# Side-by-side high and low halves in the activation tiles, and a fifth of the expert chunks loaded to two of those tiles

## The chip, the cores and the metric

The kernel runs on one core of one Trainium2 chip. The metric is the device time of one execution in microseconds (us); lower is better. Four engines do the work: TensorE (PE in the rows; its weight loads, which overlap the matmuls, are PEld), VectorE (DVE), ScalarE (ACT) and GpSimd (POOL). SyncE (SP) issues nearly all loads from HBM.

## The reference, cut to what matters

The reference is a stack of three transformer layers over 256 tokens of width 1024, all in fp32. The first two layers each mix three branches (a recurrent one, an mLSTM and attention to a memory) and end in a feed-forward part. The first of these is dense. The second is a mixture of 8 experts of which each token uses two:

```python
def swiglu(x, w1, w3, w2):            # dense; D_FF = 3584
    return (silu(x @ w1) * (x @ w3)) @ w2

# mixture: the same with w1[e], w3[e], w2[e] for the tokens sent to expert e,
# weighted by the gate and added back to their tokens
```

The third layer has two more dense feed-forward parts (width 2816) around a mixer with two kinds of attention. Every weight is used once per execution, so some 640 MB come from HBM.

## The kernel before, in words

**High and low parts.** Every fp32 matmul is made of fp32r products. A value is split into a high part (the value rounded to fp32r) and a low part (what is left). A product is high by high, plus high by low, plus low by high: three matmuls into one PSUM tile (`mm3`, lines 361 to 363).

**Weights.** They come in chunks of up to 128 x 2048 fp32, 1 MB, listed in the order of use. `run` goes through a list of steps. Each step names its chunks and a function `fn` that does its work. SP loads a chunk into a tile `w` of the pool `stream`, of which there are `RAW_BUFS` = 4 (line 317). `do_split` then casts it on ACT to the high part `wh` (line 330) and subtracts on DVE to get the low part `wl` (through `tt`, line 366). There are 3 tiles `wh` and 3 tiles `wl`. A chunk may be split up to 2 chunks ahead of the step that uses it (`look`). `load` issues the load of chunk n+4 as soon as the code has reached the split of chunk n; on the chip SP then waits until the subtraction of chunk n has read its `w`. The engines work in program order, and SP issues its loads in order.

**Activations.** They are kept with features on the partitions and the 256 tokens (`T`) along the free dimension. A tile `d` of the pool `act` (`t4k`, 4 KB a partition, 18 tiles) holds two groups of 128 features, k0 and k1, as `[P, 2, 512]`: high k0, high k1, low k0, low k1, 256 columns each. `HL` gives the two halves of such a tile, `fx` one group's high or low part.

**Three kinds of matmul groups.**
- `zmm`, `zmm_tok` and the small products use `mm3` with 256 moving columns.
- `wide` (dense feed-forward, gates, output projections) takes two matmuls a group. Line 474 has the high weights stationary and 512 moving columns, the high and the low part of one group k as `t[:, :, k*256:(k+1)*256]`: two runs of 256 columns that stand 512 columns apart. Line 476 (473 in the last group) has the low weights stationary and 256 moving columns.
- The experts (`moe_pass`) use `mm3` with the gathered tokens stationary and 512 weight columns moving, 12 matmuls a chunk. There are 8 experts x 7 blocks x 6 chunks = 336 chunks. Beside them stand the transposes (line 1349), the gathering of tokens (`prep`, lines 1297 to 1309, four times) and the scattering back (`scatter`, lines 1376 and 1377, eight times), whose sums go to `X` on DVE.

During the experts the pool of `d` tiles holds the tokens `x` (4 tiles, until the last `prep`), the gathered `xg` (4, and 8 around a `prep`), `sel`, the transposed products `ht` and the outputs `ys`.

Of the kernel before, what the change touches and what calls it, by code (L numbers as in the profile page):

```python
# [9 lines left out]
F32 = mybir.dt.float32  # L10
F32R = mybir.dt.float32r
# [3 lines left out]
OP = mybir.AluOpType  # L15
# [3 lines left out]
P = 128  # L19
# [211 lines left out]
class Step:  # L231

    look = LOOK

    def __init__(self, chunks, fn, fine=False, hold=False):
        self.chunks = chunks
        self.fn = fn
        self.fine = fine  # L240
        self.hold = hold


class HL(tuple):


    def __new__(cls, t):
        x = tuple.__new__(cls, (t[:, 0, :], t[:, 1, :]))
        x.t = t
        return x  # L250


class Kernel:
# [18 lines left out]
        return self.act.tile([P, 512], F32, name=self.name("a"), tag="a", bufs=10)  # L272

    def t4k(self, dt):
        return self.act.tile([P, 2, 512], dt, name=self.name("d"), tag="d", bufs=18)

    def pair(self):
        return HL(self.t4k(F32R))
# [1 line left out]
    def half(self, key):  # L280

        t = self.open.pop(key, None)
        if t is None:
            t = self.open[key] = self.t4k(F32)
            return t[:, 0, :]
        return t[:, 1, :]

    def t1k(self, dt=F32):
        return self.act.tile([P, 256], dt, name=self.name("b"), tag="b", bufs=6)
# [5 lines left out]
    def run(self, steps, small=False, before=lambda i, j: None):  # L295

        nc = self.nc
        flat = [c for s in steps for c in s.chunks]  # L300
        fine = [s.fine for s in steps for c in s.chunks]
        raw, split = [], []
        ns = 0

        def parts(i):
            e = flat[i].shape[-1]
            w = 512 if small or fine[i] else CHUNK
            return [slice(o, min(o + w, e)) for o in range(0, e, w)]

        def load():  # L310
            while not small and len(raw) < min(len(flat), ns + RAW_BUFS):
                ap = flat[len(raw)]
                e = ap.shape[-1]
                t = self.stream.tile([P, 2048], F32, name=self.name("w"), tag="w", bufs=RAW_BUFS)[:, :e]
                for j, s in enumerate(parts(len(raw)) if fine[len(raw)] else [slice(0, e)]):
                    before(len(raw), j)
                    nc.sync.dma_start(t[:, s], ap[:, s])
                raw.append(t)

        def do_split():  # L320
            e = flat[ns].shape[-1]
            hi, lo = (self.stream.tile([P, CHUNK], F32R, name=self.name(n), tag=n, bufs=SPLIT_BUFS)[:, :e]
                      for n in ("wh", "wl"))
            for s in parts(ns):
                if small:
                    t = self.t2k()
                    nc.sync.dma_start(t, flat[ns][:, s])
                else:
                    t = raw[ns][:, s]
                nc.scalar.copy(hi[:, s], t)  # L330
                self.tt(lo[:, s], t, hi.bitcast(F32)[:, s], OP.subtract)
            split.append((hi, lo))
            if not small:
                raw[ns] = None

        holds, n = [], 0
        for s in steps:
            if s.hold:
                holds.append(n)
            n += len(s.chunks)  # L340
        used = 0
        for s in steps:
            if s.hold:
                holds.pop(0)
            need = used + len(s.chunks)
            look = min(len(flat), need + s.look - 1, *holds[:1]) if s.chunks else 0
            load()
            while ns < look:
                do_split()
                ns += 1  # L350
                load()
            got = split[used:need]
            for i in range(used, need):
                split[i] = None
            used = need
            s.fn(*got)
# [22 lines left out]

    def split(self, src, hi, lo, scale=None):  # L380

        if scale is None:
            self.nc.scalar.copy(hi, src)
            self.tt(lo, src, hi.bitcast(F32), OP.subtract)
        else:
            self.actf(hi, src, AF.Identity, scale=scale)
            self.stt(lo, src, scale, hi.bitcast(F32), OP.mult, OP.subtract)

    def split_pair(self, src, hi, lo, scales):

        halves = [slice(m * T, (m + 1) * T) for m in range(2)]
        for s, c in zip(halves, scales):
            self.actf(hi[:, s], src[:, s], AF.Identity, scale=c)
        for s, c in zip(halves, scales):
            self.stt(lo[:, s], src[:, s], c, hi.bitcast(F32)[:, s], OP.mult, OP.subtract)

    def split2k(self, src, scale=None):
        x = self.pair()
# [64 lines left out]
    def wide(self, w, x, p, m=0, nk=DK, cols=256, koff=0, first=True, last=True):  # L463


        hi, lo = w
        for k in range(nk):
            o = k * cols + m * P
            a, z = first and k == 0, last and k == nk - 1
            xh = self.fx(x, koff + k, 0)  # L470
            xb = x[(koff + k) // 2].t[:, :, ((koff + k) % 2) * T:((koff + k) % 2 + 1) * T]
            if z:
                self.nc.tensor.matmul(p[:, :T], lo[:, o:o + P], xh, start=False, stop=False)  # L473
            self.nc.tensor.matmul(p, hi[:, o:o + P], xb, start=a, stop=z)  # L474
            if not z:
                self.nc.tensor.matmul(p[:, :T], lo[:, o:o + P], xh, start=False, stop=False)  # L476
        return p
# [145 lines left out]
    def mixer(self, l):  # L623
# [153 lines left out]
        def uchunk(c):  # L777
            def fn(w):
                p = self.zmm(w, S["h"])
                uh, ul = S["u", c] = self.pair()  # L780
                nc.scalar.copy(uh, p)
                y = conv(p, c, "conv_ml_w", "conv_ml_b")
                self.tt(ul, p, uh.bitcast(F32), OP.subtract)
                th = self.t2k()
                self.actf(th, y, AF.Tanh, scale=0.5)
                self.stt(y, th, 1.0, y, OP.add, OP.mult)
                S["c", c] = self.split2k(y)
            return step([wz(2, c)], fn)
# [481 lines left out]
    def moe_pass(self, R, base, tail=None):  # L1270
# [4 lines left out]
        def prep(pr):  # L1275
            def fn():
                sel = self.pair()[0]
                pos, mk = R["pos"], R["mk"]
                io = self.c("iota")
                for t in range(2):  # L1280
                    for j in range(2):
                        e = 2 * pr + j
                        o = sel[:, t * T + j * P:t * T + (j + 1) * P]
                        if base:
                            sh = self.small(1)
                            self.ts(sh, pos[:, t * 8 + e:t * 8 + e + 1], -float(base), None, OP.add)
                        else:
                            sh = pos[:, t * 8 + e:t * 8 + e + 1]
                        self.ts(o, io, sh, mk[:, t * 8 + e:t * 8 + e + 1], OP.is_equal, OP.mult)
                x = R["x"]  # L1290
                xg = [h for _ in range(DK // 2) for h in self.pair()]
                for k in range(DK):
                    p = self.psum()
                    q, o = k // 4, (k % 4) * P
                    for i in range(2):
                        for t in range(2):
                            nc.tensor.matmul(p[:, i * T:(i + 1) * T], x[t][q][i][:, o:o + P],  # L1297
                                             sel[:, t * T:(t + 1) * T], start=t == 0, stop=t == 1)
                    nc.scalar.copy(xg[k], p)
                for j in range(2):  # L1300
                    e = 2 * pr + j
                    S["xg", e] = xg
                    p = self.psum()
                    for t in range(2):
                        s = sel[:, t * T + j * P:t * T + (j + 1) * P]
                        nc.tensor.matmul(p[:, :T], s, self.pad[:, t, :], start=t == 0, stop=t == 1)
                    for t in range(2):
                        s = sel[:, t * T + j * P:t * T + (j + 1) * P]
                        nc.tensor.matmul(p[:, T:T + 16], s, R["gs"][:, t, :], start=t == 0, stop=t == 1)
                    st = self.t1k(F32R)  # L1310
                    nc.scalar.copy(st, p[:, :T])
                    gt = self.small(1)
                    gh = self.small(1)
                    nc.vector.tensor_copy(gh, p[:, T + 8 + e:T + 9 + e])
                    self.tt(gt, p[:, T + e:T + e + 1], gh, OP.add)
                    S["st", e], S["gt", e] = st, gt
            return Step([], fn)
# [91 lines left out]
        seq += [tr(*prev), down(*prev, 0), down(*prev, 1), scatter(N_EXP - 1)]  # L1409
        for s in seq:  # L1410
            s.look = SPLIT_BUFS
        return seq


# [424 lines left out]
```

## Time and profile before

| | |
|---|---|
| time, median of 3 runs | 2769.58 us (2769.38 to 2773.06) |
| the profiled execution's own time | 2771.64 us |
| its span, first to last instruction | 2769.5 us |
| PE, DVE, ACT busy | 98%, 80%, 61% of the span |
| mean granted TensorE clock | 0.994 |
| the experts' stage | about 1060 to 2057 us |

The profile is that of one execution. "Busy" is the time in which an engine had an instruction under way. PE's matmuls are pipelined, so their recorded lengths overlap (a 512-column matmul is recorded with some 0.39 us while the next one starts 0.23 us later); how fast PE goes is read from one start to the next. "a <- b" in a wait means that a stood still until b was done. The rows that the prediction rests on stand in a section of their own below.

### The profile page before, as it was taken

The page shows a single profiled execution, that of the slowest core. Times are in us where ns is not written, and L with a number is a line of the kernel's source. Part 1 is how long each engine was busy: PE and PEld are TensorE (multiplying, and loading weights), DVE is VectorE, ACT ScalarE, POOL GpSimd, SP SyncE. Part 2 cuts the span into 40 slices and gives each one's busy share as a digit, 9 for nine tenths or more (in the row PEclk, how much of TensorE's full clock was granted, in tenths as well). Part 3 has the DMA queues.
Part 4 walks back from the last instruction along what each step waited for, and adds up shares of the span by engine and source line. Part 5 has one row for each costly group of instructions (what it writes and reads, how often), then busy time and mean ns, then how long its engine had stood idle before and what let it go on. Part 6 is the DMA issues. An engine that isn't in the chain of part 4 may idle for free.

```text
span 2769.5 us, 40041 instructions
## 1 busy us (share of the span) xinstructions
PE 2708.6 (98%) x16234; PEld 2380.9 (86%) x16234; DVE 2213.7 (80%) x2723; ACT 1682.4 (61%) x1851; POOL 8.9 (0%) x20
## 2 busy tenths in 40 slices
PE   8999999999999998999999999999999999999998
PEld 8999988889999997788788777887778889989887
DVE  7787778866797768888998989898988766777885
ACT  6665555544665546777776777777775544565553
POOL 0000000000000000000000000000000000000000
PEclk9999999999999998999999999999999999999999
DMA  6454445555445446999999999999984554434543
GB/s 262 150 178 164 152 179 183 178 203 178 158 177 178 139 147 251 361 345 351 360 352 336 349 358 348 347 349 360 350 330 152 178 203 174 173 111 163 188 155 119
DMA packets 96219, 649.84 MB, mean 235 GB/s; under 512 B 11552, under 2 KB 11808, under 8 KB 24224
## 3 DMA queue, kind: packets, MB, share of 16 engines
q1 hardware_dynamic: 94464, 642.54, 64.0%
q0 software_dynamic: 1280, 4.20, 0.4%
q8 instruction: 128, 2.10, 0.3%
q14 instruction: 59, 0.48, 0.1%
q10 hardware_dynamic: 288, 0.52, 0.1%
HBM read 646.17 MB, written 1.05 MB: 234 GB/s over the span
## 4 chain that ended last, share of the span: by engine, by line
PE 40%; DMA 10%; DVE 7%; ACT 4%; issue 2%; ACTq 0%; DVEq 0%
PE ps L474 10%; DMA w<-in_mw 10%; PE ps L362 7%; PE ps L361 7%; PE ps L363 7%; DVE wl L366 6%; PE ps L476 5%; ACT wh L330 3%; PE ps L1297 1%; PE ps L473 1%; PE ps L1349 0%; DVE X L366 0%; ACT d L378 0%; DVE a L369 0%; PE ps L1536 0%
## 5 line engine op out<-in xcount | busy, mean ns | idle before, releaser
L366 DVE TENSOR_TENSOR wl<-w,wh 128x2048 fp32r<-128x2048 f32 (+4 forms) x635 | 1390.1, 2198 | 275.9 <-ACT wh L330 273.7
L330 ACT CAST wh<-w 128x2048 fp32r<-128x2048 f32 (+4 forms) x635 | 1166.5, 1839 | 577.3 <-issue 192.3
L474 PE MATMUL ps<-d,wh 128*128 128x512 f32 x2560 | 896.0, 399 | 1.9 <-DVE d L369 1.9
L476 PE MATMUL ps<-d,wl 128*128 128x256 f32 x2288 | 643.2, 281 | 0.0
L362 PE MATMUL ps<-wl,d 128*128 128x512 f32 (+1 forms) x1616 | 615.9, 381 | 7.4 <-DVE wl L366 5.2
L363 PE MATMUL ps<-wh,d 128*128 128x512 f32 (+1 forms) x1616 | 601.9, 373 | 3.1 <-DVE d L369 3.1
L361 PE MATMUL ps<-wh,d 128*128 128x512 f32 (+1 forms) x1616 | 603.9, 374 | 0.0
L474 PEld LDWEIGHTS ps<-d,wh 128*128 128x128 f32 x2560 | 468.4, 189 | 96.0 <-DVE d L369 3.7
L361 PE MATMUL ps<-d,wh 128*128 128x256 f32 (+1 forms) x1536 | 438.3, 286 | 10.8 <-ACT wh L330 10.8
L476 PEld LDWEIGHTS ps<-d,wl 128*128 128x128 f32 x2288 | 434.0, 190 | 10.0 <-DVE wl L366 0.2
L363 PE MATMUL ps<-d,wl 128*128 128x256 f32 (+1 forms) x1536 | 435.6, 284 | 0.0
L362 PE MATMUL ps<-d,wh 128*128 128x256 f32 (+1 forms) x1536 | 435.5, 284 | 0.0
L362 PEld LDWEIGHTS ps<-wl,d 128*128 128x128 f32 x1616 | 304.5, 188 | 89.1 <-DVE wl L366 40.9
L361 PEld LDWEIGHTS ps<-wh,d 128*128 128x128 f32 x1616 | 304.5, 188 | 54.6 <-ACT d L378 0.2
L363 PEld LDWEIGHTS ps<-wh,d 128*128 128x128 f32 x1616 | 304.9, 189 | 51.9 <-DVE d L369 3.7
L361 PEld LDWEIGHTS ps<-d,wh 128*128 128x128 f32 (+1 forms) x1536 | 293.4, 191 | 12.1 <-ACT wh L330 10.8
L362 PEld LDWEIGHTS ps<-d,wh 128*128 128x128 f32 (+1 forms) x1536 | 293.7, 191 | 1.0
L363 PEld LDWEIGHTS ps<-d,wl 128*128 128x128 f32 (+1 forms) x1536 | 293.5, 191 | 0.7 <-DVE wl L366 0.2
L484 ACT COPY a<-ps 128x256 f32<-128x256 f32 x144 | 53.1, 369 | 170.1 <-PE ps L474 169.9
L366 DVE TENSOR_TENSOR a<-ps,a 128x256 f32<-128x256 f32 (+1 forms) x146 | 61.1, 421 | 45.1 <-ACT a L484 44.9
L366 DVE TENSOR_TENSOR d<-ps,d 128x256 f32<-128x256 f32 (+3 forms) x152 | 75.9, 515 | 17.4 <-ACT d L484 14.2
L369 DVE SCALAR_TENSOR_TENSOR d<-ps,d 128x512 fp32r<-128x512 f32 (+1 forms) x104 | 62.8, 604 | 19.6 <-PE ps L474 19.0
(217 smaller groups left out, 2020.2 us busy)
## 6 DMA issues: line engine op xcount, KB each, us to landing
w<-in_mw SPq DMA_DIRECT2D x334, 1024.0 KB, 7.0
w<-in_wz SPq DMA_DIRECT2D x64, 1024.0 KB, 4.8
w<-in_win SPq DMA_DIRECT2D x32, 1024.0 KB, 4.8
w<-in_f0w SPq DMA_DIRECT2D x28, 1024.0 KB, 4.8
w<-in_wbr SPq DMA_DIRECT2D x24, 1024.0 KB, 4.8
w<-in_f1w SPq DMA_DIRECT2D x22, 1024.0 KB, 4.8
w<-in_f2w SPq DMA_DIRECT2D x22, 1024.0 KB, 4.8
w<-in_wkv SPq DMA_DIRECT2D x15, 1024.0 KB, 4.9
```

Source lines behind the costliest of these rows:

```text
L330: nc.scalar.copy(hi[:, s], t)
L361: mm(out, lh, rh, start=first, stop=False)
L362: mm(out, lh, rl, start=False, stop=False)
L363: mm(out, ll, rh, start=False, stop=last)
L366: self.nc.vector.tensor_tensor(out=out, in0=a, in1=b, op=op)
L369: self.nc.vector.scalar_tensor_tensor(out, a, s, b, op0=op0, op1=op1)
L473: self.nc.tensor.matmul(p[:, :T], lo[:, o:o + P], xh, start=False, stop=False)
L474: self.nc.tensor.matmul(p, hi[:, o:o + P], xb, start=a, stop=z)
L476: self.nc.tensor.matmul(p[:, :T], lo[:, o:o + P], xh, start=False, stop=False)
L484: self.nc.scalar.copy(o, p[:, T:])
L1297: nc.tensor.matmul(p[:, i * T:(i + 1) * T], x[t][q][i][:, o:o + P], sel[:, t * T:(t + 1) * T], start=t == 0, stop=t == 1)
```

## The change

It has two parts.

1. **Layout.** A tile `d` becomes `[P, 1024]`, ordered high k0, low k0, high k1, low k1. The 512 moving columns of line 474 are then one run. The high half as a whole, which ACT and DVE write in one instruction, becomes two runs of 256 columns (`Half.all()`); single groups stay one run. Gathered tiles `xg` keep the order they had.
2. **Twin chunks.** Among the 336 expert chunks, each with index 9, 14, 19, ... 319 (63 of them) is loaded not to a tile `w` but to two tiles `d`, by two loads of 512 KB, and split in two halves of 1024 columns. `load` may now have four plain chunks and one twin chunk ahead of the split.

```diff
@@ class Step
+    twin = False
+class Half:
+    def __init__(self, t, i):
+        self.t, self.i = t, i
+    def __getitem__(self, at):
+        p, s = at
+        a, z = s.start or 0, s.stop or 2 * T
+        o = a // T * T + self.i * T
+        return self.t[p, a + o:z + o]
+    def all(self):
+        return self.t.rearrange("p (k h t) -> p k h t", k=2, h=2)[:, :, self.i, :]
 class HL(tuple):
-        x = tuple.__new__(cls, (t[:, 0, :], t[:, 1, :]))
+        x = tuple.__new__(cls, (Half(t, 0), Half(t, 1)))
+class Twin:
+    def __init__(self, tiles):
+        self.tiles = tiles
+    def __getitem__(self, at):
+        s = at[1]
+        i = s.start // 1024
+        return self.tiles[i][:, s.start - i * 1024:s.stop - i * 1024]
@@ t4k
-        return self.act.tile([P, 2, 512], dt, name=self.name("d"), tag="d", bufs=18)
+        return self.act.tile([P, 1024], dt, name=self.name("d"), tag="d", bufs=18)
@@ run
+        twin = [s.twin for s in steps for c in s.chunks]
-            w = 512 if small or fine[i] else CHUNK
+            w = 512 if small or fine[i] else 1024 if twin[i] else CHUNK
 ...
-            while not small and len(raw) < min(len(flat), ns + RAW_BUFS):
-                ap = flat[len(raw)]
+            while not small and len(raw) < len(flat):
+                i = len(raw)
+                if twin[ns:i].count(twin[i]) >= (1 if twin[i] else RAW_BUFS):
+                    break
+                ap = flat[i]
                 e = ap.shape[-1]
-                t = self.stream.tile([P, 2048], F32, name=self.name("w"), tag="w", bufs=RAW_BUFS)[:, :e]
-                for j, s in enumerate(parts(len(raw)) if fine[len(raw)] else [slice(0, e)]):
-                    before(len(raw), j)
+                if twin[i]:
+                    t = Twin([self.t4k(F32) for _ in range(2)])
+                else:
+                    t = self.stream.tile([P, 2048], F32, name=self.name("w"), tag="w", bufs=RAW_BUFS)[:, :e]
+                for j, s in enumerate(parts(i) if fine[i] or twin[i] else [slice(0, e)]):
+                    before(i, j)
                     nc.sync.dma_start(t[:, s], ap[:, s])
@@ split
+        if isinstance(hi, Half):
+            src, hi, lo = src.rearrange("p (k t) -> p k t", k=2), hi.all(), lo.all()
@@ wide
-            xb = x[(koff + k) // 2].t[:, :, ((koff + k) % 2) * T:((koff + k) % 2 + 1) * T]
+            xb = x[(koff + k) // 2].t[:, ((koff + k) % 2) * 512:((koff + k) % 2 + 1) * 512]
@@ moe_pass, prep
-                xg = [h for _ in range(DK // 2) for h in self.pair()]
+                xg = [t[:, i * 512:(i + 1) * 512] for t in [self.t4k(F32R) for _ in range(DK // 2)] for i in range(2)]
@@ moe_pass, end
+        for i, s in enumerate([s for s in seq if s.chunks]):
+            s.twin = i % 5 == 4 and 4 < i < 320
```

## Rows read from the trace of the kernel before

**Rows 1.** The page: busy us (share of the span) and instructions of each engine

```profile
PE 2708.6 (98%) x16234; PEld 2380.9 (86%) x16234; DVE 2213.7 (80%) x2723; ACT 1682.4 (61%) x1851; POOL 8.9 (0%) x20
```

**Rows 2.** The experts' stage: us, PE, PEld, DVE, ACT, POOL busy, PE clock, DMA share, GB/s

```profile
1060.00:2057.00 997.00, 988.50 (x4469) 794.40 (x4469) 884.64 (x578) 718.74 (x499) 0.00 (x0) 1.00 0.95 352
```

**Rows 3.** Waits, 1060 to 2057 us: us in total, times, longest us

```profile
ACT wh L330 <- DMA w<-in_mw: 186.2, 180, 2.8
DVE wl L366 <- ACT wh L330: 82.7, 125, 2.4
PEld ps L362 <- DVE wl L366: 40.9, 95, 1.2
```

**Rows 4.** Waits of SP's own queue, 1060 to 2057 us

```profile
SPq L317 <- DVE wl L366: 852.9, 331, 7.7
```

**Rows 5.** Timeline around 1620 us: start, length, what [idle before <- releaser]

```profile
1614.69 0.39 PE L362 MATMUL ps<-wl,d 128*128 128x512 f32 x1
...
1618.15 1.91 ACT L330 CAST wh<-w 128x2048 fp32r<-128x2048 f32 x1 [2.43 <-DMA w<-in_mw]
...
1621.27 0.39 PE L361 MATMUL ps<-wh,d 128*128 128x512 f32 x1
1622.44 0.19 PEld L362 LDWEIGHTS ps<-wl,d 128*128 128x128 f32 x1 [1.21 <-DVE wl L366]
...
1622.78 0.39 PE L363 MATMUL ps<-wh,d 128*128 128x512 f32 x1
```

**Rows 6.** DMA issues: count, KB each, median us from issue to landing

```profile
w<-in_mw SPq DMA_DIRECT2D x334, 1024.0 KB, 7.0
...
w<-in_wa SPq DMA_DIRECT2D x4, 512.0 KB, 3.2
```

**Rows 7.** One short stretch of the same table of stages

```profile
1373.50:1383.60 10.10, 10.10 (x47) 8.34 (x46) 9.68 (x6) 8.60 (x6) 0.00 (x0) 1.00 0.99 395
```

**Rows 8.** Weight splits by shape, whole span: count | busy us, mean ns | idle before

```profile
L366 DVE TENSOR_TENSOR wl<-w,wh 128x2048 fp32r<-128x2048 f32 x561 | 1278.9, 2289 | 216.8 <-ACT wh L330 215.2
L330 ACT CAST wh<-w 128x2048 fp32r<-128x2048 f32 x561 | 1072.5, 1912 | 467.9 <-DMA w<-in_mw 186.2 <-issue 140.6 <-PE ps L362 77.1
...
L366 DVE TENSOR_TENSOR wl<-w,wh 128x512 fp32r<-128x512 f32 x12 | 7.5, 684 | 0.0
```

**Rows 9.** Matmuls by shape, whole span, same columns

```profile
L474 PE MATMUL ps<-d,wh 128*128 128x512 f32 x2560 | 896.0, 399 | 1.9 <-DVE d L369 1.9
L476 PE MATMUL ps<-d,wl 128*128 128x256 f32 x2288 | 643.2, 281 | 0.0
...
L361 PE MATMUL ps<-wh,d 128*128 128x512 f32 x1344 | 526.2, 392 | 0.0
L363 PE MATMUL ps<-wh,d 128*128 128x512 f32 x1344 | 524.9, 391 | 1.3 <-DVE d L369 1.3
...
L363 PE MATMUL ps<-d,wl 128*128 128x256 f32 x1520 | 431.1, 284 | 0.0
```

**Rows 10.** Timeline, dense stage: first and last of 11 starts of line 474

```profile
600.02 0.40 PE L474 MATMUL ps<-d,wh 128*128 128x512 f32 x1
...
603.55 0.40 PE L474 MATMUL ps<-d,wh 128*128 128x512 f32 x1
```

**Rows 11.** Timeline, zmm stage: first and last of 27 starts

```profile
99.80 0.28 PE L362 MATMUL ps<-d,wh 128*128 128x256 f32 x1
...
102.92 0.28 PE L361 MATMUL ps<-d,wh 128*128 128x256 f32 x1
```

**Rows 12.** Activations with plain and with broken or repeated runs, by shape

```profile
L366 DVE TENSOR_TENSOR a<-a,b 128x512 f32<-128x512 f32 x72 | 48.9, 690 | 1.8
L366 DVE TENSOR_TENSOR a<-a,a 128x512 f32<-128x512 f32 x65 | 44.5, 687 | 1.5
...
L378 ACT ACTIVATE d<-X,prm 128x256 f32<-128x256 f32 x16 | 9.4, 615 | 1.2 <-DVE X L366 1.2
L378 ACT ACTIVATE d<-a,prm 128x256 fp32r<-128x256 f32 x16 | 6.9, 502 | 0.3 <-DVE a L366 0.3
```

More of the change, by code (lines that the diff above doesn't have):

```diff
@@ L284, in half @@
             t = self.open[key] = self.t4k(F32)
-            return t[:, 0, :]
-        return t[:, 1, :]
+            return t[:, 0:512]
+        return t[:, 512:1024]
     def t1k(self, dt=F32):
@@ L394, in split_pair @@
         for s, c in zip(halves, scales):
-            self.stt(lo[:, s], src[:, s], c, hi.bitcast(F32)[:, s], OP.mult, OP.subtract)
+            self.stt(lo[:, s], src[:, s], c, hi[:, s].bitcast(F32), OP.mult, OP.subtract)
     def split2k(self, src, scale=None):
@@ L780, in fn @@
                 uh, ul = S["u", c] = self.pair()
-                nc.scalar.copy(uh, p)
+                p3 = p.rearrange("p (k t) -> p k t", k=2)
+                nc.scalar.copy(uh.all(), p3)
                 y = conv(p, c, "conv_ml_w", "conv_ml_b")
-                self.tt(ul, p, uh.bitcast(F32), OP.subtract)
+                self.tt(ul.all(), p3, uh.all().bitcast(F32), OP.subtract)
                 th = self.t2k()
```

## Prediction

> **What bounds the kernel now.** I read the page's busy times first. PE is busy in 98% of the span, DVE in 80% [rows 1], so a gain has to come out of PE: either its matmuls get shorter, or a wait of it goes away. The table of stages then singles out the experts: 997 us in which the DMA engines are busy for 95% at 352 GB/s and DVE for 884.6 us, 89% [rows 2]. Three resources stand close together there, so I asked for the waits of that stage. In them a weight load of PE stands before the first low-part matmul of a chunk (line 362) until the subtraction has made `wl`: 95 times, 40.9 us. The subtraction stood for the cast 125 times, 82.7 us. The cast stood for the load 180 times, 186.2 us [rows 3]. The chain thus goes back to the loads; and in SP's own queue the loads stand for the subtraction, 331 times and 852.9 us, because it frees their `w` [rows 4]. The stage is a ring of four buffers. A load takes 7.0 us to land [rows 6], the cast 1.91 and the subtraction 2.29 [rows 8], together 11.2 us. Four chunks at the stage's pace of 997 / 336 = 2.97 us last 11.9. That leaves 0.7 us, so a late load is felt at once. The bandwidth isn't used up: in one stretch of 10 us the loads ran at 395 GB/s [rows 7], which is 1.0486 MB / 395 = 2.65 us a chunk against 2.97.
>
> **What the waits cost PE.** From 1614.69 to 1621.27 us thirty matmuls start, 0.227 us apart. Then a cast that had stood 2.43 us for its load makes `wl` late: the weight load stands 1.21 us, and the next start comes 1.17 us after the last, 0.94 late. The one after it comes after 0.34 instead of 0.227, another 0.11 late [rows 5]. So a wait costs PE its length less 0.27, plus 0.11. Over the 95 waits that is 40.9 - 95 x 0.16 = 25.7 us. This is the most that earlier chunks can give.
>
> **Change, part 2: twin chunks.** Indices 9 to 319 in steps of 5 make 63 chunks. Adds: 63 more load issues on SP, which mostly stands still [rows 4]; 63 more casts; 63 more subtractions. The fixed part of a subtraction follows from two sizes, (2289 - 684) / 1536 = 1.045 ns a column and 2289 - 2048 x 1.045 = 149 ns [rows 8]. DVE gets 63 x 0.149 = 9.4 us more in a stage where it idles 997 - 884.6 = 112 us, 82.7 of them before a late cast. ACT gets 63 more casts in a stage where it is busy 719 of 997 us [rows 2]. If a half cast took as long as a whole one, that would be 63 x 1.91 = 120 us of 278 idle ones [rows 8], and at the other end nothing; I cost it at nothing, since two halves of a size that runs this long come nearer to one whole, and PE isn't waiting for ACT as such but for the load before it. In return a twin's subtraction of the first half can start after half a cast.
>
> Moves: in the order of SP a twin follows a plain load directly and needs no `w`. With chunks 9 and 14 as twins, load 13 waits for the subtraction of 8 as before, 14 goes right behind it, and 15 waits for that of 10 (before: 11). Every load thus starts about one chunk earlier, and the ring has 5 x 2.97 = 14.8 us for its 11.2. A load will take longer to land, as more are under way; by the 2.65 us a chunk [rows 7] it can't fall behind 2.97. The twin's tiles come from the 18 tiles `d`. By the names that the experts use, 4 (`x`) + 4 (`xg`) + 1 or 2 (`ht`) + up to 2 (`ys`) live at once, 15 around a `prep`, and a twin adds 2 to 4: room everywhere but at the three `prep`s inside the stage, where a writer may wait for a subtraction that is already in DVE's queue. I cost that at nothing; 3 waits like that of [rows 5], 1.05 us each, would be 3 us.
>
> How much of the 25.7 us goes? The bounds are all of it, and below nothing the 9.4 us of DVE. What stays is the part that isn't the loads' doing: after a `scatter` DVE has four sums for `X` in its queue ahead of the next subtractions, and look-ahead ends with the 3 tiles `wl`. Of the 125 waits of DVE for a cast, not all, but most, lie behind one of the 180 waits for a load [rows 3]. I take half, 12 us, less a fifth of DVE's 9.4, 2: **10 us gained**, range -24 to +9.
>
> [...] The trace has 512 KB loads, landing after 3.2 us when little else is under way [rows 6]. [...]
>
> **Change, part 1: layout.** It removes no instruction. What may change is the pace of line 474. Its 512 columns in two runs last 399 ns in the records; the experts' 512 columns in one run last 392 and 391. The 256 columns of line 476 last 281, those of `zmm` 284 [rows 9]. These lengths overlap by about the same amount, so their differences are differences of pace: (399 - 391.5) + (281 - 284) = 4.5 ns a pair. The starts say the same: ten pairs of the dense stage take 3.53 us, 353 ns each [rows 10]; one run of 512 and one of 256 would be 227 [rows 5] + 120 (26 steps in 3.12 us) [rows 11] = 347, so 6 ns. With 2560 pairs, that is 11.5 to 15 us if the break between the runs is the cause. A pair also differs from both comparisons by its mix of lengths, so a part may stay: I take 4 ns, **10 us gained**, between nothing and 15. Nothing hides it: PE is the engine that is always busy.
>
> The cost is on ACT and DVE, which now write the whole high or low half in two runs of 256. No row shows that. The nearest are a DVE operation whose operand repeats after 256 columns, 690 ns against 687, and an ACT operation that writes with a step in runs of a few elements, 615 against 502 for 256 columns [rows 12]. I take the first, 3 ns, as two long runs are nearest to it; some 230 such pairs of operations, counted in the code, make under 1 us, beside PE. At the other end 2 x 113 ns on 230 would be 52 us of ACT's 1087 idle.
>
> [...]
>
> **The sum.** The profiled execution's own time is 2771.6 us; 2771.6 - 10 - 10 = 2751.6. The median of the runs is 2.1 below that execution, so I forecast 2749.5, say **2750 us**.
>
> **Rivals.** (a) The layout gives nothing; the loads do their part: 2760. For it: both runs are long, and the excess could come from alternating 512 and 256 columns. Against it: 512 columns take longer there than anywhere else. (b) The loads come earlier but PE waits as often, since the order on DVE (subtractions behind products that stand for PE) sets `wl`; the layout works: 2760. (c) DVE becomes the bound. It does 884.6 + 9.4 us of work in a stage of 997; the point is where the 30 us of its idle time that no cast causes are used up, first in the blocks with a `scatter`, where six subtractions (13.7 us) and seven more passes over 512 columns (0.68 each [rows 8]) nearly fill the time of 72 matmuls (16.3) and the scatter's own. Then the 9.4 us lie on the path: 2769.6 + 9.4 = 2779 without a gain from the layout, 2769 with it. Against it: most of DVE's idle time follows late casts. (d) The change doesn't do what it says: loads go out earlier but wait in the same queue, the stage stays as it is, and the layout gives nothing: 2770.
>
> **How the numbers follow.** Forecast 0.42, (a) 0.28, (b) 0.10, (c) slower 0.08, (c) even 0.06, (d) 0.06. About 0.2%, 5.5 us, is what a measurement of this kernel can tell from no change. Faster takes the forecast, four fifths of (a), since the loads' gain may be under 5.5, and nearly all of (b): 0.42 + 0.22 + 0.09 = 0.73. Same takes the rest of these and the even cases: 0.19. Slower: 0.08. Both ceilings together would give 2769.6 - 25.7 - 15 = 2729, which I think unlikely; from 2738 up to 2769 the range leaves out the slower case and the end of the forecast, about 2 in 10.
>
> **What would show it.** Line 474 at 392 ns instead of 399: the layout works; still 399: rival (a). In the experts' stage, waits of casts for loads well under 186 us and of PE's weight loads under 25, with the stage near 987 us: the ring was the cause. Those of the casts gone and PE's still near 41: rival (b). The subtractions without idle time before them and the stage at or over 997: rival (c). A load that lands 7 us after its issue, as now, with SP still standing for the fourth chunk back: rival (d). The forecast is wrong at its base if PE's time between waits, 0.227 us a matmul, changes in the experts' stage.

## The result and the profile after

| | before | after |
|---|---|---|
| time, median | 2769.48 us (2767.75 to 2773.06) | 2807.67 us (2807.07 to 2812.74) |
| ratio | | 1.014, 95% interval 1.0123 to 1.0158 |
| span of the profiled execution | 2769.5 us | 2805.3 us |
| mean granted TensorE clock | 0.994 | 0.987 |

The change makes the kernel 38 us slower; 2750 us had been forecast, with 2738 to 2769 as the range. In the code of after, `mm3` is lines 400 to 402, the cast 369, the subtraction (`tt`) 405, the other DVE passes over a product (`stt`) 408, the copies and activations of ACT 417, the load 356 and the wide matmuls 515 and 517.

The table of stages (columns as in [rows 2]) gives the place of the loss. Ahead of the experts nothing has changed: PE is busy for 994.35 us of the first 1010 before and 994.19 after. The experts' stage ends some 38 us later.

```profile
0.00:1010.00 1010.00, 994.19 (x7059) 928.07 (x7060) 780.92 (x1238) 575.14 (x792) 0.20 (x4) 1.00 0.50 177
1060.00:2095.00 1035.00, 992.50 (x4467) 810.17 (x4466) 889.74 (x641) 723.40 (x561) 0.00 (x0) 0.98 0.90 338
```

Beside [rows 2]: the stage does the same matmuls (x4467 against x4469) in 1035 us instead of 997. PE stands idle for 42.5 us of it instead of 8.5, and the granted clock is 0.98 instead of 1.00. The bandwidth fell from 352 to 338 GB/s, and DVE, with 889.7 of 1035 us, is further from being the bound than before.

The waits of that stage, in the columns of [rows 3]:

```profile
ACT wh L369 <- PE ps L402: 233.6, 247, 8.4
DVE wl L405 <- ACT wh L369: 114.6, 153, 6.7
...
PEld ps L400 <- ACT wh L369: 17.8, 12, 2.4
PEld ps L401 <- DVE wl L405: 16.2, 20, 2.1
PEld ps L402 <- DVE d L408: 16.0, 9, 2.8
...
PEld ps L400 <- ACT d L417: 9.7, 8, 2.9
```

The casts' waits for loads, 186.2 us in [rows 3], are gone from the list. They now stand for PE to give a `wh` free: the loads do come earlier, as the change meant. PE's 95 short waits for `wl` have become 20. In their place stand long ones, at ten places of the stage: seven times 2.4 us for a cast and three times 2.9 us for the high half of the transposed products (line 417 writes `d`). At seven of these places a second wait follows, of 1.4 to 2.8 us, for their low half (line 408), and at one a wait of 2.1 us for `wl`. The rest of the counts above are mostly waits of 0.2 to 1.3 us.

**One such place.** ACT and DVE around 1115 us (start, length, what, [idle before <- releaser]):

```profile
1109.67 0.60 ACT L417 ACTIVATE a<-ps 128x512 f32<-128x512 f32 x1 [1.20 <-PE ps L402]
1110.17 1.90 ACT L369 CAST wh<-w 128x2048 fp32r<-128x2048 f32 x1
...
1112.39 1.92 ACT L369 CAST wh<-w 128x2048 fp32r<-128x2048 f32 x1 [0.32 <-PE ps L402]
...
1115.11 1.90 ACT L369 CAST wh<-w 128x2048 fp32r<-128x2048 f32 x1 [0.80 <-PE ps L402]
...
1115.72 4.49 DVE L405 TENSOR_TENSOR wl<-w,wh 128x2048 fp32r<-128x2048 f32 x2
1116.92 0.59 ACT L417 ACTIVATE d<-ps 128x512 fp32r<-128x512 f32 x1
...
1120.12 0.68 DVE L408 SCALAR_TENSOR_TENSOR d<-ps,d 128x512 fp32r<-128x512 f32 x1
1123.46 1.91 ACT L369 CAST wh<-w 128x2048 fp32r<-128x2048 f32 x1 [5.96 <-PE ps L402]
```

and PE in the same microseconds:

```profile
1114.46 0.39 PE L401 MATMUL ps<-wl,d 128*128 128x512 f32 x1
1114.68 0.39 PE L402 MATMUL ps<-wh,d 128*128 128x512 f32 x1
1117.06 0.79 PE L400 MATMUL ps<-wh,d 128*128 128x512 f32 x1 [1.99 <-ACT wh L369]
...
1118.93 0.63 PE L401 MATMUL ps<-wl,d 128*128 128x512 f32 x1
1119.36 0.63 PE L400 MATMUL ps<-wh,d 128*128 128x512 f32 x1
1120.86 0.50 PE L402 MATMUL ps<-wh,d 128*128 128x512 f32 x1 [0.87 <-DVE d L408]
1121.20 0.39 PE L400 MATMUL ps<-wh,d 128*128 128x512 f32 x1
```

ACT casts three chunks between the tanh (1109.67) and the copy of the transposed products (1116.92). PE, which the plan sends to a chunk of the next block meanwhile, stands for the third of these casts until 1117.06. On DVE two whole subtractions (4.49 us from 1115.72) stand ahead of the low half of that copy, which starts at 1120.12; PE stands for it until 1120.86. PE's starts are 2.38 and 1.50 us apart at the two gaps, where 0.227 is usual: 3.4 us lost. The last two starts between them are 0.43 us apart. The stretch from 1117 to 1121 has a granted clock of 0.57:

```profile
1114.00:1117.00 3.00, 1.07 (x5) 0.56 (x3) 2.28 (x3) 2.20 (x3) 0.00 (x0) 1.00 0.99 384
1117.00:1121.00 4.00, 3.07 (x9) 2.07 (x10) 3.81 (x3) 0.51 (x2) 0.00 (x0) 0.57 0.86 313
1121.00:1125.00 4.00, 4.00 (x18) 3.30 (x19) 0.00 (x0) 1.53 (x1) 0.00 (x0) 1.00 0.95 356
```

4 us x (1 - 0.57) is another 1.7 us at most, as part of the second gap lies in this stretch. Ten such places start at 1114.68, 1207.32, 1301.88, 1394.18, 1487.88, 1580.65, 1673.58, 1767.66, 1866.38 and 1958.60 us. They come about every 93 us, which is 30 chunks: the twins come every 5 chunks, the experts' block has 6. They are not alike. Two (1301.88 and 1487.88) have one long gap, the other eight two, of up to 2.88 and 2.73 us from start to start. The granted clock falls at eight (read in stretches of 1 us, to 0.50 at each of them), but not at 1487.88 and 1958.60, where it is 1.00, though the gaps there are 2.38 us and 2.38 and 2.56 us:

```profile
1487.00:1497.00 10.00, 7.45 (x33) 5.44 (x32) 6.24 (x5) 4.03 (x4) 0.00 (x0) 1.00 0.97 347
1958.00:1968.00 10.00, 5.85 (x27) 4.27 (x26) 6.00 (x5) 3.25 (x4) 0.00 (x0) 1.00 0.95 359
```

At 3.4 + 1.7 us each the ten would make some 51 us (a rough estimate from the first alone). The stage's rows give the same size: 42.5 - 8.5 = 34 us more idle time, and a clock of 0.98 in 1035 us, 21 us, together 55. That is against a stage without such places; what it would be like, the experiments show.

**What orders the engines.** The description ahead of the prediction says that the engines work in program order, and the prediction builds on the order of the program text. That is not so. A planner fills the queue of each engine when the program is built, and it may put a later step's cast ahead of an earlier step's copy, as the three casts from 1110.17 us above. What comes first is then waited for: with ACT held (experiment 3) DVE idles 4.30 us, until 1122.43, for PE's product, though the cast for a subtraction behind it (from 1117.60, 1.91 us) is done at 1119.51. How the planner chooses, no run here shows. The traces show what it chose. In the text, the copy of the transposed products stands right behind a tanh, at 55 places of the stage. In the trace of the kernel before, ACT has four casts of chunks (two halves counted as one) between the two at 29 of these places, more at 11 and none at 15. In the changed kernel it has none at 22, one at 10, two at 7, three at ten and more at 6; the ten with three (after the tanh at 1109.7, 1200.3, 1296.4 and so on to 1953.6 us) are those just ahead of the ten waits. PE, too, goes back and forth: at 19 places at least it begins a chunk, does matmuls of another and then goes on with the first; in the kernel before at three.

### The profile page after: what moved, and what is told of

Its sections match the earlier page's. It is cut to its first block, busy times and chain, and to the rows that moved or that the text cites. A ratio compares the mean times of both kernels' runs of the same rounds, so it can differ in the third digit from the quotient of the medians.

```text
span 2805.3 us, 40250 instructions
## 1 busy us (share of the span) xinstructions
PE 2710.7 (97%) x16234; PEld 2395.0 (85%) x16234; DVE 2218.4 (79%) x2786; ACT 1687.5 (60%) x1914; POOL 8.9 (0%) x20
## 4 chain that ended last, share of the span: by engine, by line
PE 56%; DVE 4%; ACT 2%; issue 1%; DVEq 0%; ACTq 0%
PE ps L402 13%; PE ps L401 13%; PE ps L400 12%; PE ps L515 10%; PE ps L517 5%; DVE wl L405 3%; ACT wh L369 1%; PE ps L1391 1%; PE ps L1339 1%; PE ps L514 1%; ACT d L417 0%; DVE d L408 0%; PE ps L1580 0%; PE ps L479 0%; PE ps L1624 0%
## 5 line engine op out<-in xcount | busy, mean ns | idle before, releaser
L405 DVE TENSOR_TENSOR wl<-w,wh 128x2048 fp32r<-128x2048 f32 (+5 forms) x572 | 1247.7, 2189 | 301.1 <-ACT wh L369 299.8
L369 ACT CAST wh<-w 128x2048 fp32r<-128x2048 f32 (+5 forms) x572 | 1045.9, 1831 | 539.6 <-issue 192.3
L401 PE MATMUL ps<-wl,d 128*128 128x512 f32 (+1 forms) x1616 | 609.4, 377 | 8.1 <-DVE wl L405 8.0
L405 DVE TENSOR_TENSOR wl<-d,wh 128x1024 fp32r<-128x1024 f32 x126 | 148.5, 1219 | 6.2 <-ACT wh L369 6.1
L369 ACT CAST wh<-d 128x1024 fp32r<-128x1024 f32 x126 | 126.5, 1053 | 42.8 <-PE ps L402 42.8
```

The source lines that it names most:

```text
L401: mm(out, lh, rl, start=False, stop=False)
L405: self.nc.vector.tensor_tensor(out=out, in0=a, in1=b, op=op)
```

## Experiments

Every time is a median; the ratio behind it, with its 95% interval, is to the kernel before on the same chip, which took 2770 to 2774 us there.

**1. The two parts by themselves.** The layout alone: the changed kernel with

```diff
-            s.twin = i % 5 == 4 and 4 < i < 320
+            s.twin = False
```

> The changed kernel with no twin chunk: the layout alone. Theory 'order' (the twin chunks alter the order in which the program issues work to PE, ACT and DVE in the experts' stage, and the layout does nothing, since line 474 has its 399 ns as before): 2769 to 2772 us, line 474 (here 515) at 399 ns, experts' stage 997 us. Rival 'layout' (writing a half in two runs costs ACT and DVE): near 2808. Rival 'both' (the layout gains 10 us that the twins hide): 2760.

2771.81 us, 0.9997 (0.9987 to 1.0007). The matmul that the layout was to shorten:

```profile
L515 PE MATMUL ps<-d,wh 128*128 128x512 f32 x2560 | 897.1, 400 | 1.9 <-DVE d L408 1.9
```

400 ns, and 399 in the whole change, as in [rows 9]. The layout is worth nothing. The twins alone, with the old layout (tiles `[P, 2, 512]`, a twin using them as a flat 1024 columns):

> The kernel before with the 63 twin chunks alone, activation tiles in the old layout. Theory 'order': 2806 to 2810 us, the same ten or so waits of PE over 1 us in the experts' stage as with the whole change. Rival 'layout': 2770.

2810.19 us, 1.0126 (1.0109 to 1.0143): the whole loss is the twins'.

**2. Halved, but not earlier.** The whole change, but a twin's two halves go to one tile `w`, four chunks ahead as before:

```diff
-                if twin[ns:i].count(twin[i]) >= (1 if twin[i] else RAW_BUFS):
+                if i >= ns + RAW_BUFS:
                     break
...
-                if twin[i]:
-                    t = Twin([self.t4k(F32) for _ in range(2)])
-                else:
+                if True:
                     t = self.stream.tile([P, 2048], F32, name=self.name("w"), tag="w", bufs=RAW_BUFS)[:, :e]
```

> The changed kernel, but the 63 chunks go to ordinary tiles w with four chunks ahead as before; they are still loaded and split in two halves. Theory 'order': without the fifth buffer the order on PE stays that of the program, block after block, so no waits over 1 us; time within 2765 to 2780. Rival 'halves' (the cost is in 63 more loads, casts and subtractions, at most 63 x 0.15 on DVE and 63 x 0.19 on ACT, and in smaller loads): 2790 to 2808.

2771.0 us, 0.9988 (0.9978 to 0.9998). The 63 more loads, casts and subtractions cost nothing that shows. Waits of over 1 us had been ruled out, and there are a few: three gaps of PE, of 2.16, 1.87 and 1.39 us from start to start (at 1309.52, 1446.78 and 1565.42 us), all for `wl`.

```profile
PEld ps L399 <- DVE wl L403: 35.7, 66, 2.1
```

But the granted clock of 1060 to 2095 us is 0.99 there, against 0.98 in the changed kernel, and the ten places don't come. They take the fifth buffer.

**3. The order of the text held.** Edges that only order (`NoSync` in the kernel) tie each operation of an engine to the one before it in the text, throughout the experts' stage:

```diff
+            if s.look == SPLIT_BUFS:
+                self.pin(begin, (E.PE, E.Activation, E.DVE,))
...
+    def pin(self, start, engines):
+        bb = self.nc.cur_bb.bb.instructions
+        last = self.pinned
+        for i in bb[start:]:
+            if i.engine in engines:
+                if i.engine in last:
+                    self.tc.add_manual_dep(
+                        i, last[i.engine].name,
...
+                last[i.engine] = i
```

First on all three engines, with the whole change:

> The whole change, with PE, ACT and DVE held to the order of the program text in the experts' stage by order-only edges (no added waits). Theory 'order': the waits over 1 us go, the earlier loads do their part, the clock stays at 1.00: 2750 to 2770 us, stage 980 to 997. Rival 'halves' or 'pool' (twin tiles make others wait for a tile d): still 2800 to 2810.

2758.58 us, 0.9942 (0.9925 to 0.9958). ACT now has no cast between the tanh and the copy at any of the 55 places. Two of PE's waits for `wl` are left in the stage, 2.3 us in all. Of the longer ones, three ahead of the gathering of tokens are left (2.6 us of idle time each), and some at the two ends of the stage. The twins' tiles `d` are the same here, so it isn't a want of tiles that makes the ten places. Then the same edges in the kernel before:

> The kernel before with the order of the program text held on PE, ACT and DVE in the experts' stage, four buffers and no twin. It tells how much of e4's gain is order and how much the fifth buffer. Theory 'buffer' (the earlier loads take away the waits for wl): about 2780, since the three waits of 2.8 us before the gathering that e4 shows come on top of the 40 us of waits of before. Rival 'order alone': 2758 as e4.

2769.71 us, 0.9992 (0.9975 to 1.0008), between the two times that had been expected. So the held order is worth nothing without the twins, and with it the twins are worth 2769.7 - 2758.6 = 11 us (14 by the two ratios). Next, the changed kernel with one or two engines in that list. PE alone, `(E.PE,)`:

> The whole change with the order of the program text held on PE alone; ACT and DVE keep the order the planner gives them. Theory 'PE order' (what costs is that PE meets a chunk of the next block before the one it needs): near e4's 2758. Rival 'ACT and DVE order' (what costs is that casts and subtractions stand ahead of the copy of the transposed products): waits of PE over 1 us remain, 2785 to 2808.

2827.15 us, 1.0203 (1.0183 to 1.0222). Worse: PE now stands in the text's order for copies that ACT still makes late.

```profile
PEld ps L416 <- ACT d L433: 26.2, 9, 2.9
```

ACT and DVE, `(E.Activation, E.DVE,)`, with PE left to the planner:

> The whole change with the order of the program text held on ACT and DVE alone. Theory 'PE order': PE still goes back and forth between chunks, 2785 to 2808. Rival 'ACT and DVE order': near e4's 2758.

2753.61 us, 0.9935 (0.9916 to 0.9955). PE's order needed no holding. PE still goes back and forth at 16 places, as here, where it begins a chunk, does another one and goes on with the first at 1125.56, but it stands for no more than 1.3 us at any of them:

```profile
1122.61 0.61 PE L416 MATMUL ps<-wh,d 128*128 128x512 f32 x2
1123.06 0.39 PE L417 MATMUL ps<-wl,d 128*128 128x512 f32 x1
...
1125.33 0.39 PE L418 MATMUL ps<-wh,d 128*128 128x512 f32 x1
1125.56 0.39 PE L417 MATMUL ps<-wl,d 128*128 128x512 f32 x1
```

The stage:

```profile
1060.00:2050.00 990.00, 978.56 (x4504) 809.85 (x4504) 899.48 (x647) 731.36 (x568) 0.00 (x0) 1.00 0.94 357
```

4504 matmuls in 990 us, against 4469 in 997 [rows 2], at clock 1.00. Which of the two queues matters? ACT alone, `(E.Activation,)`:

> The whole change, with the order of the program text held on ACT alone; DVE and PE are ordered by the planner. Theory: the subtractions of a chunk need its cast, so a held ACT keeps the casts of later chunks behind the copies of the transposed products and with them most of the subtractions; time near that with both held (2753.6), 2748 to 2770, and PE's waits of over 2 us every 93 us are gone. Rival, DVE's queue is the one that matters (it copies the low halves of the transposed products behind two subtractions): 2790 to 2808, the waits of 2 us stay.

2802.62 us, 1.011 (1.0093 to 1.0128). DVE alone, `(E.DVE,)`:

> The whole change, with the order of the program text held on DVE alone; ACT and PE are ordered by the planner. Theory (ACT's queue matters): ACT still casts later chunks ahead of the copies, so PE goes on waiting for them as in the changed kernel, 2790 to 2815. Rival, DVE's queue matters: 2748 to 2770, no waits of 2 us.

2841.69 us, 1.0255 (1.0238 to 1.0272). The theory, that ACT's order decides, falls: each alone is no cure. The place around 1122 us shows why. DVE with ACT held:

```profile
1117.45 0.68 DVE L424 SCALAR_TENSOR_TENSOR a<-a,ps 128x512 f32<-128x512 f32 x1
1122.43 0.69 DVE L421 TENSOR_TENSOR a<-a,ps 128x512 f32<-128x512 f32 x1 [4.30 <-PE ps L418]
1123.03 0.68 DVE L424 SCALAR_TENSOR_TENSOR d<-ps,d 128x512 fp32r<-128x512 f32 x1
1123.63 4.48 DVE L421 TENSOR_TENSOR wl<-w,wh 128x2048 fp32r<-128x2048 f32 x2
```

and with DVE held:

```profile
1123.14 0.69 DVE L424 SCALAR_TENSOR_TENSOR d<-ps,d 128x512 fp32r<-128x512 f32 x1 [6.70 <-ACT d L433]
1123.75 4.48 DVE L421 TENSOR_TENSOR wl<-w,wh 128x2048 fp32r<-128x2048 f32 x2
```

In the first, DVE has the product that belongs ahead of the transposes in front of two subtractions, and idles 4.30 us for PE's up products; PE then waits 3.1 us for `wl`. In the second, DVE is in order and idles 6.70 us for a copy that ACT has put behind three casts. Each queue here passes on the lateness of the other one, 4.30 us in the first run and 6.70 in the second.

**4. Which part of the order, and what sets it off.** Only the copies of the transposed products held: the casts and subtractions that the text has behind such a copy stay behind it.

```diff
+                n = len(nc.cur_bb.bb.instructions)
                 nc.scalar.copy(hi[:, s], t)
                 self.tt(lo[:, s], t, hi.bitcast(F32)[:, s], OP.subtract)
+                for i in nc.cur_bb.bb.instructions[n:]:
+                    if i.engine in self.copies:
+                        self.tc.add_manual_dep(
+                            i, self.copies[i.engine].name,
...
+                n = len(self.nc.cur_bb.bb.instructions)
                 S["ht", e, f] = self.split2k(p, 0.5)
+                self.copies = {i.engine: i for i in self.nc.cur_bb.bb.instructions[n:]}
```

> The changed kernel (every fifth chunk) with one thing held on ACT and DVE: the casts and subtractions that the text has behind the copy of the transposed products stay behind it. All else is ordered by the planner. Theory, the place of these copies is all that matters: as with the whole order held on both (2753.6), 2748 to 2765. Rival, the rest of the two orders matters too (the product before the transposes on DVE, which stalled when ACT alone was held): waits of 3 us stay, 2790 to 2808.

2795.34 us, 1.009 (1.0072 to 1.0107). The rival holds. In the trace no cast stands between the tanh and the copy at 50 of 55 places, but PE still waits at 3.52 us from start to start at nine places some 93 us apart, and again it is DVE's product ahead of the subtractions:

```profile
DVE a L413 <- PE ps L410: 47.4, 17, 4.3
```

Then no order held, but every sixth chunk a twin, so that the twin always takes the same place in a block:

```diff
-            s.twin = i % 5 == 4 and 4 < i < 320
+            s.twin = i % 6 == 2 and 4 < i < 320
```

> The changed kernel with every sixth chunk instead of every fifth in two activation tiles, so that the chunk so loaded always takes the same place in a block of six: the last up chunk but one of the block's first half (numbers 8, 14, 20). No order is held. In the plan ACT copies the transposed products behind five casts of chunks after the tanh that stands ahead of them in the text, in 27 of 44 places (four casts in the kernel before, nought to three in turn in the changed kernel). Theory, the waits come where the planner puts the copies later than PE needs them: now they come in most blocks of 18.6 us instead of every 93 us, 2800 to 2950. Rival, the waits come of the varying place itself (every fifth chunk against blocks of six): they vanish, 2750 to 2765.

2760.82 us, 0.9962 (0.995 to 0.9975). With `i % 6 == 1`, the place at which the waits of the changed kernel stand:

> As the run with every sixth chunk, but one chunk earlier in the block (numbers 7, 13, 19). In the plan the copies stand behind four casts in 27 of 44 places, as in the kernel before. Theory (the planner's late copies make the waits): as the plan has the pattern of the kernel before, no wait of over 2 us of PE recurs, and the earlier loads show: 2748 to 2765. Rival, a chunk in activation tiles at this place of the block is what makes the wait (in the changed kernel each of the waits every 93 us stands right behind the chunk that takes this place): a wait in each block, 2850 or more.

2765.11 us, 0.9976 (0.9966 to 0.9985). In neither do the waits of over 2 us recur, but for three of 2.6 us ahead of the gathering in the second and those at the end of the stage. So it is not a place in the block that is bad, and not a late copy as such (in the first, five or six casts stand ahead of it at 33 of 55 places). What is left is that the place varies: every fifth chunk against blocks of six. The other four places were not run, and these two kernels also have fewer twins (52 and 53 for 63). PE's waits for `wl` in the first of these runs:

```profile
PEld ps L401 <- DVE wl L405: 23.9, 36, 0.9
```

40.9 us and 95 waits were those of [rows 3].

**5. A faster version, and what the fifth buffer is worth in it.** The selection matrices are made one block ahead of their gathering, as a step of their own, and the order is held on all three engines but for the first three and the last four steps of the stage:

```diff
+        def sels(pr):
...
+                if f == 2 and e % 2 and e < N_EXP - 1:
+                    seq.append(sels((e + 1) // 2))
                 if f == 3 and e % 2 and e < N_EXP - 1:
                     seq.append(prep((e + 1) // 2))
...
+        for s in seq[3:-4]:
+            s.pin = True
```

> e4 with the selection matrices of the gathering (four DVE operations) made one block earlier and the order left free at both ends of the stage. If the three waits of 2.8 us and the clock that falls after them are what e4 still loses there (3 x 2.8, and about as much again at half the clock, and 4 us at the ends): 2742 to 2750 us. If the waits only move: 2756 to 2760.

2740.27 us (2739.81 to 2742.77), 0.9892 (0.9872 to 0.9911): faster than both kernels. The same without twins (`s.twin = False`):

> The kernel with the order held on PE, ACT and DVE inside the experts' stage and the selection matrices made one block earlier (2740.3), but without the chunks that are loaded to two activation tiles: four chunk buffers as in the kernel before. Theory: the earlier loads are worth what they were forecast to free once the order is held, 10 to 25 us, so 2750 to 2766, with waits of PE's weight loads for the subtraction's result back at 19 us or more. Rival, the gain comes of the held order and the earlier selection matrices alone: 2738 to 2744.

2754.3 us, 0.993 (0.991 to 0.995). The fifth buffer is worth 14 us there (11 by the two ratios), as the theory had it. As the held order alone was worth nothing without twins (2769.7 us), the rest, 15 us (17 by the two ratios), comes with the earlier matrices and the free ends, which the runs don't part further. Without the twins the waits for loads and for `wl` are back:

```profile
ACT wh L371 <- DMA w<-in_mw: 98.0, 98, 2.9
...
PEld ps L419 <- DVE wl L423: 17.6, 40, 1.5
```

**6. Why 399 ns.** The kernel before takes 512 and 256 columns in turn through a group of 8 to 14 pairs, and only in the last pair 256 comes first. The edit puts all matmuls of 512 columns of a group first and all of 256 after them (the text below speaks of two and two, which holds for the end of a group alone):

```diff
-        for k in range(nk):
-            o = k * cols + m * P
 ...
+        at = [k * cols + m * P for k in range(nk)]
+        for k, o in enumerate(at):
 ...
-            self.nc.tensor.matmul(p, hi[:, o:o + P], xb, start=a, stop=z)
+            self.nc.tensor.matmul(p, hi[:, o:o + P], xb, start=first and k == 0, stop=False)
+        for k, o in enumerate(at):
+            self.nc.tensor.matmul(p[:, :T], lo[:, o:o + P], self.fx(x, koff + k, 0), start=False, ...)
```

> The kernel before, with one edit in the loop of the wide matmuls: the two of 512 columns first, then the two of 256, instead of 512, 256, 256, 512. It asks where the 399 ns of the 512-column matmul of this line come from, against 391 and 392 ns on the lines of the other groups. Theory, they come of the order of the two lengths: the mean moves from 399 by 4 ns or more, and by 2560 matmuls the time moves by some 10 us in the same direction. Rival, they come of the reads of the weights or of the products' place: 398 to 400 ns and 2767 to 2773 us.

2779.78 us, 1.0033 (1.0014 to 1.0051), and 397 ns (line 470): neither bound is met. A group in the dense stage, fourteen of each:

```profile
600.92 1.83 PE L472 MATMUL ps<-d,wl 128*128 128x256 f32 x14
602.60 3.36 PE L470 MATMUL ps<-d,wh 128*128 128x512 f32 x14
```

In the dense stage it did gain: 573 matmuls in the 100 us where the kernel before has 568. It lost in other stages, as from 300 to 400 us:

```profile
300.00:400.00 100.00, 93.97 (x638) 87.11 (x637) 70.75 (x132) 48.41 (x63) 0.00 (x0) 0.97 0.42 148
500.00:600.00 100.00, 100.00 (x573) 87.83 (x572) 75.34 (x93) 52.93 (x66) 0.00 (x0) 1.00 0.56 195
```

The kernel before, in the same stretches:

```profile
300.00:400.00 100.00, 97.82 (x677) 90.18 (x677) 77.09 (x145) 51.00 (x67) 0.00 (x0) 1.00 0.44 158
500.00:600.00 100.00, 100.00 (x568) 86.83 (x568) 75.02 (x88) 50.59 (x65) 0.00 (x0) 1.00 0.54 186
```

So the order of lengths makes some 3 ns of a pair (0.9% of 353); where the rest of the excess comes from, the runs leave open.

## Why the prediction was wrong

**What bounds the stage: right.** The ring of four buffers did make PE's short waits. With a fifth buffer the casts' 186.2 us of waiting for loads are gone in the whole change, and with the order held so are all but two of PE's waits for `wl`. One slip in the working changes nothing: before, load 13 waited for the subtraction of chunk 9, not 8, so it moves by one chunk like the others. Whole loads don't take longer to land: 6.1 us in the median, 7.0 before [rows 6].

**The costs of part 2: right.** A subtraction of a half takes 1219 ns, so that two cost 148 ns more than a whole one; 149 had been worked out:

```profile
L405 DVE TENSOR_TENSOR wl<-w,wh 128x2048 fp32r<-128x2048 f32 x498 | 1136.6, 2290 | 242.0 <-ACT wh L369 241.3
...
L405 DVE TENSOR_TENSOR wl<-d,wh 128x1024 fp32r<-128x1024 f32 x126 | 148.5, 1219 | 6.2 <-ACT wh L369 6.1
...
L369 ACT CAST wh<-d 128x1024 fp32r<-128x1024 f32 x126 | 126.5, 1053 | 42.8 <-PE ps L402 42.8
```

Two half casts cost 2 x 1053 - 1912 = 194 ns more, 12 us of ACT in all, near the lower of the two ends given. Experiment 2 shows that none of it reaches the end.

**The step that failed: "Every load thus starts about one chunk earlier".** That is true of the loads, and the sum went on as if all else kept its place. It had the order of the text for the order of the engines, and asked only whether each wait that is there now gets shorter. But with the fifth buffer the planner ordered ACT, DVE and PE anew in the whole stage, by the counts of casts above, and PE got ten places with long waits. The cost is 2807.7 - 2753.6 = 54 us between the changed kernel and the same with ACT and DVE held (57 by the two ratios). This fits ten places at 5.1 us each. The 10 us forecast for the earlier loads are what they give where the order is steady: 11 to 14 us with all three engines held and in the fastest version, 11 and 7 (by the ratios) with a twin in every sixth place. That term was the half of 25.7 us less 2, and the half was a choice, so that it comes so close is partly luck.

**The rivals.** Rival (b) said that DVE's order sets `wl`, and priced it at no gain; the place was half right, the size wrong, since it too took that order as fixed. Rival (c), DVE as the bound, was on the slower side for another reason: DVE has more idle time after the change (145 us of the stage, 112 before), and experiment 2 does its 9.4 us of work for nothing. Rival (d) is out, since the casts' waits for loads are gone. No rival had an order that gets worse.

**The term for the layout: 10 us forecast, nothing measured.** This is rival (a). The comparison of 399 with 391.5 ns was sound as far as it went, but it set a pair of lengths in one group against pairs in others, and the break between the runs wasn't the only thing that differs there. The differences that were read as a gain had another explanation at hand, the mix of lengths, named in the text itself. The traces show no difference: 399 and 400 ns with one run (the whole change, the layout alone), 399 with two [rows 9].

The cost of that term, 3 ns a pair of operations and 113 ns for each at the other end, is nothing too. No operation that writes a half in two runs has become longer by more than 3 ns. Two of them, before and after:

```profile
L383 ACT CAST d<-a 128x512 fp32r<-128x512 f32 x45 | 27.6, 619 | 56.9 <-DVE a L366 29.8 <-DVE a L369 27.0
L366 DVE TENSOR_TENSOR d<-a,d 128x512 fp32r<-128x512 f32 x45 | 30.5, 687 | 6.0 <-ACT d L383 5.4
...
L424 ACT CAST d<-a 128x512 fp32r<-128x512 f32 x45 | 27.6, 619 | 56.9 <-DVE a L405 29.8 <-DVE a L408 27.0
L405 DVE TENSOR_TENSOR d<-a,d 128x512 fp32r<-128x512 f32 x45 | 30.5, 687 | 6.0 <-ACT d L424 5.4
```

**Halved loads.** In the changed kernel the halves land 7.4 us after their issue, in the queue with the other loads. Experiment 2, with 126 loads of 512 KB in the experts' stage, takes 0.9988 of the time before, so halving costs nothing that shows, in loads that SP issues one behind the other.

## What to carry to other kernels

Where a planner fills the queues, a change of a buffer can also be a change of order, as the fifth buffer was here; ask of each engine what comes in its queue directly ahead of the work that PE needs next, and whether a period of the change (here 5) meets a period of the loop (here 6). If waits recur at their common multiple, hold the order on the engines that feed PE, on all of them at once: here one held queue only moved the wait into the next. And price a layout by rows of the same instruction mix before taking a few nanoseconds times thousands.

## What the runs showed of the hardware

At most of the ten places a gap in PE's work cost more than its length. After 2.38 us without a start at 1114.68 us, matmuls start 0.43 us apart at a granted clock of 0.57 in the mean of 4 us (0.50 in the 2 us from 1117.68), and are back at 0.23 and 1.00 after that. The clock falls like that, to 0.50, at eight of the ten. At the other two, with gaps of 2.38 us, and of 2.38 and 2.56 us, it stays at 1.00, so the runs give no length of gap from which on it falls. A wait of 1.21 us in the kernel before was followed by 0.34 and then 0.23 from start to start [rows 5], at a granted clock of 1.00. So ten places with one or two longer waits each, some 51 us, are dearer here than the 95 short waits of [rows 3], 25.7 us at the most.

A write in two runs of 256 fp32r columns took as long as one of 512 in one run: 619 ns on ACT and 687 on DVE either way.
